# Sums with V in runs of four behind each key product, turned keys at the other end of memory, and seven banks for the mixer's output in one hybrid decoder step

## The chip, the cores and the metric

The kernel runs on one core of a Trainium2 chip. The metric is device time in microseconds (us), the median of several executions. Engines are named as in the profile: PE is TensorE, PEld its weight loads, DVE VectorE, ACT ScalarE, POOL GpSimd, SP SyncE, which here only issues DMAs. A page of the paged cache in this text means one gather of [128, 1024] floats (512 KB).

## The reference

One layer of a decoder for two request groups, 1024 prompt tokens and 8 samples of 8 new tokens each (64 more columns, 1088 together), all in float32. Cut to what matters for the change:

```python
h = x + 0.5 * rms_norm(swiglu(rms_norm(x)))                    # FFN1
q_sb, k_sb, v_sb, q_r, k_r, v_r, g_r, a_sb, a_r = split(rms_norm(h) @ w_in)
o_sb = stick_breaking(q_sb, k_sb, v_sb)                        # 8 heads x 64, strictly causal
o_r  = silu(g_r) * head_rms_norm(retention(rope(q_r), rope(k_r), v_r))
m = sigmoid(a_sb) * (o_sb @ w_sb_out) + sigmoid(a_r) * (o_r @ w_ret_out)
h = h + rms_norm(m @ w_o)
h = h + 0.5 * rms_norm(swiglu(rms_norm(h)))                    # FFN2

def sb_block(q, k, v, ...):        # a sample sees 2048 cached keys (16 pages of 128) and its new ones
    z = q k^T / 8 + bias
    log_stay = where(mask, log_sigmoid(-z), 0)
    a = where(mask, exp(log_sigmoid(z) + sum of log_stay of all later keys), 0)
    return a @ v
```

The samples' keys and values come through a page table from the pools `cache_k` and `cache_v`, 8 samples x 2048 keys x 512 floats each, 67 MB for both.

## The kernel before

Everything is kept with features on partitions and the 1088 tokens as columns. A dense product is done as three matmuls (`mm3`, L133, L137, L138), with each operand split into a high part (`hi`, L96, on ACT) and a low part (`lo`, L99, on DVE, for some weights on POOL). The program runs FFN1, the combined projection `w_in`, retention, the prompt's stick-breaking attention (`prompt_sb`), the samples' attention (`decode_sb`), the mixer's output (`mixer_out`) and FFN2.

**Samples' attention.** Four groups `g` of two samples (`b2`). For each group, blocks `j` of 512 cached keys are taken from last to first. `gather` (L1100, on POOL) brings two pages of keys per sample and block; they are turned on PE by 16 transposes (L1202, four per `m`) and copied by DVE or ACT (L1207, L1209) into `kt`, one of two tiles in pool `deck`. `product` (L1183, matmuls at L1115) multiplies them with the queries `qd`, which lie block by block in 32 columns with zeros between. `stick` (L1139 to L1158) makes the weights, `weights` (L1174) turns them on PE into `at`. `values` (L1226) then sums these with V: one call per 128 keys, two calls to a page of V. A call of `side_by_side` (L1111) is four matmuls on 32 columns each, which stand next to each other in the array, one per pair of heads; PE's instructions list a call as "32x128 x4", and the trace as one row of "128*32 ... x8" or more. Key products are such calls too, with 512 columns.

**What sets the order.** The code is written as generators, and each `yield` is a place where other work may be put. `both` takes a step of the keys of group g+1 and a step of the values of group g in turn, one V call to a step; `through` adds dense work at each step, `FILL_DEC` pieces of `fill` for each (`fill(1)` is one k of three matmuls). The dense work is what `a_r`'s gates and `o_r @ w_ret_out` need (L866, `ret_steps`, operands `uh`, `ul` and weights `wh`, `wl`). Its operands `ul` are loaded from `orT` in `ret_prep` (L843). A scheduler then places the instructions of each engine by their readiness and priority; three of a call's four matmuls have a high priority and follow the first. SP issues all plain DMAs in one order, and POOL all gathers, along with memsets and some low parts.

**Memory.** Pools are opened and closed like a stack. The pages lie in pool `decp`, the turned keys in `deck`, both opened after `prompt_sb` has closed all of its pools, the one of the prompt's keys and values (`pqk`) with them, and both closed before `mixer_out` opens its own.

**Mixer.** The outputs of both attentions lie in DRAM (`osT`, all 1088 columns, and `orT`). `mixer_out` (L1511) loads `osT` into `sq` (L1528) in chunks of 512, 288 and 288 columns, makes high and low parts, multiplies with `w_sb_out` into one of two banks "pa", and DVE multiplies by the gate `gaT` (L1542, L1545) and adds the retention's share `mrT` (L1544, L1546). The scheduler mixes these with the products by `w_o` (banks "pb"). The last lines of `decode_sb` store the samples' part into `osT` (L1275).

Of the kernel before, what the change touches and what calls it, by code (L numbers as in the profile page):

```python
# [43 lines left out]
FILL_DEC = (.6, .8, .8, .8, .6)  # L44
# [24 lines left out]
class Trunk:  # L69
# [99 lines left out]
    def setup(self):  # L169
# [17 lines left out]
        self.osT = self.t(self.dram, [512, T], "osT")  # L187
# [700 lines left out]
    def prompt_sb(self):  # L888
        nc, io = self.nc, self.io
        win = io["w_in"][0]  # L890
        with ExitStack() as ctx:
            qp = self.pool("pqk", ctx)
# [12 lines left out]
            def proj(p):  # L905

                qs = [self.t(qp, [P, TP], "qs", F32R, bufs=3) for e in range(2)]
                kh = [self.t(qp, [P, TP], "kh", F32R, bufs=3) for e in range(2)]
                kl = [self.t(qp, [P, TP], "kl", F32R, bufs=3) for e in range(2)]
                vs = [self.t(qp, [P, 8, P], "vs", F32R, bufs=3) for e in range(2)]  # L910
# [159 lines left out]
    def decode_sb(self):  # L1070
# [5 lines left out]
        with ExitStack() as ctx:  # L1076
            pp = self.pool("decp", ctx)
            kp_ = self.pool("deck", ctx)
            dp = self.pool("dec", ctx)
# [11 lines left out]
            kn = self.t(kp_, [P, 4, TD], "kn")  # L1091
# [13 lines left out]
            qd = self.t(kp_, [P, 288], "qd")  # L1105
            nc.gpsimd.memset(qd, 0.0)
            atns = [self.t(dp, [P, P], f"atn{x}") for x in range(2)]
            for x in range(2):
                nc.gpsimd.memset(atns[x][64:128], 0.0)

            def side_by_side(out, w, x, first, last):  # L1111
# [13 lines left out]
            def logits(g, ats):  # L1125


                qv = qd.rearrange("q (b x) -> q b x", x=144)[:, :, :P].rearrange("q b (m y) -> q b m y", y=32)
# [31 lines left out]
                def new_keys():  # L1160
# [4 lines left out]
                    bt = self.t(dp, [P, TD], "btn")  # L1165
# [5 lines left out]
                    nc.scalar.activation(atn[:TD], tp[:TD, :P], AF.Copy)  # L1171
# [11 lines left out]
                def product(ps, b2, j, kt):  # L1183
                    side_by_side(ps, partial(query, b2), lambda m: kt[:, m, :], b2 == 0, b2 == 1)
                    if b2:
                        bt = self.t(dp, [P, 512], "bt", bufs=2)
                        left[0] = stick(bt, ps.rearrange("q (h i x) -> q h x i", h=2, i=2), 512, left[0])
                        todo.append((j, bt))

                late, todo, left = [], [], [None]  # L1190
                nk = new_keys()
                step = 0
                for j in range(NG - 1, -1, -1):
                    ps = self.bank("pb")
                    for b2 in range(2):
                        kp = [gather(self.t(pp, [P, 1024], "page", bufs=6), ck, 2 * g + b2, 2 * j + x)
                              for x in range(2)]
                        kt = self.t(kp_, [P, 4, 512], "kt", bufs=2)
                        for m in range(4):
# [6 lines left out]
                            if m % 2:  # L1206
# [3 lines left out]
                            if late and m == 1:  # L1210
                                product(*late.pop(0))
                            if todo and b2 == 1:
                                weights(*todo.pop(0))
# [4 lines left out]
                        late.append((ps, b2, j, kt))  # L1218
                while late:
                    product(*late.pop(0))  # L1220
                yield
                while todo:
                    weights(*todo.pop(0))
                yield

            def values(g, ats):  # L1226
                po = self.bank("pm")
                for b2 in range(2):
                    out = po[:, b2 * P : (b2 + 1) * P]
                    for j in range(NG, -1, -1):  # L1230
                        for i in range(4 if j < NG else 1):
                            if j < NG and i % 2 == 0:
                                vp = gather(self.t(pp, [P, 1024], "vpage", bufs=5), cv, 2 * g + b2, 2 * j + i // 2)
# [3 lines left out]
                                               lambda m: src[:, m * P : (m + 1) * P], j == NG, j == 0 and i == 3)  # L1237
                            self.marks.append(ins.ins)
# [13 lines left out]
            def both(k, v):  # L1252
                for _ in range(2):
                    next(k)
                    yield
                done = False
                while not done:
                    done = True
                    for x in (k, v):
                        if next(x, x) is not x:  # L1260
# [573 lines left out]
```

## Time and profile before

| what | value |
|---|---|
| median of 3 runs | 2899.72 us (2897.93 to 2901.84) |
| profiled execution, its own time | 2891.72 us |
| its span | 2889.2 us |
| mean granted PE clock | 0.99 |
| PE busy | 2798.6 us, 97% |
| DVE, ACT, POOL busy | 70%, 43%, 26% |
| samples' attention | about 1641 to 1942 us |
| first mixer product | 1947.88 us |

The span is the time from the first to the last recorded instruction of the profiled execution; its own time is that of the same execution as the runs are timed, and differs from the median as executions differ. PE's matmuls are pipelined: one starts before the row of the one before it ends, so what a matmul costs is read from start to start, not from its length. PEclk is the share of PE's full clock that was granted in a stretch.

### The profile page before, as it was taken

What the parts mean: (1) busy time and instruction counts of PE and PEld (TensorE: products, weight loads), DVE (VectorE), ACT (ScalarE), POOL (GpSimd) and SP (SyncE); (2) the same over time, 40 slices, a digit from 0 to 9 for tenths busy, and PEclk for the clock granted to TensorE, in tenths of its full rate; (3) what the DMA queues carried; (4) which work ended last, traced back from release to release, by engine and by line L of the source; (5) the groups of instructions that cost most, each with busy time, mean ns of one, the idle gap of its engine ahead of it and who ended that gap; (6) DMA issues with size and microseconds to landing.
All of it is one profiled execution on the core that took longest, in us unless ns stands there. A gap on an engine that the chain in (4) does not pass through costs nothing.

```text
span 2889.2 us, 51617 instructions
## 1 busy us (share of the span) xinstructions
PE 2798.6 (97%) x20064; PEld 2633.3 (91%) x20064; DVE 2017.1 (70%) x3922; ACT 1245.3 (43%) x2546; POOL 738.5 (26%) x679
## 2 busy tenths in 40 slices
PE   7999999999999999999999889989999999999998
PEld 7898899999999999989999867768989988999997
DVE  7888878888753553546888744436578888688776
ACT  6444444444343333335666543213354444544443
POOL 0234513333150000000000245520013334233321
PEclk9999999999999999999999999999999999999999
DMA  6444444333252322333222389876333336333431
GB/s 177 145 127 144 140 155 123 110 112 108 80 162 83 99 84 86 94 113 80 76 74 76 123 294 332 297 244 198 105 96 121 119 110 189 122 103 107 130 89 42
DMA packets 420420, 380.63 MB, mean 132 GB/s; under 512 B 30352, under 2 KB 380944, under 8 KB 420176
## 3 DMA queue, kind: packets, MB, share of 16 engines
q1 hardware_dynamic: 397904, 306.03, 34.6%
q0 software_dynamic: 22272, 71.31, 7.4%
q8 instruction: 157, 2.57, 0.4%
q14 instruction: 87, 0.71, 0.1%
HBM read 310.03 MB, written 63.05 MB: 129 GB/s over the span
## 4 chain that ended last, share of the span: by engine, by line
PE 59%; DVE 5%; DMA 3%; issue 2%; POOL 1%; ACT 1%; SPq 0%; DVEq 0%; POOLq 0%; ACTq 0%
PE pa L133 10%; PE pa L138 10%; PE pa L137 10%; PE pb L133 3%; PE pb L138 3%; PE pb L137 3%; PE pc L137 3%; PE pc L138 3%; PE pc L133 3%; PE pc L1202 2%; PE pm L1011 1%; PE pm L1115 1%; PE pc L999 1%; DVE sl L99 1%; DMA ul<-orT 1%
## 5 line engine op out<-in xcount | busy, mean ns | idle before, releaser
L96 ACT ACTIVATE sh<-wr 128x512 fp32r<-128x512 f32 x592 | 340.0, 624 | 364.1 <-POOL wr L590 135.5
L133 PE MATMUL pa<-uh,wh 128*128 128x384 f32 (+1 forms) x1408 | 476.7, 339 | 4.2 <-ACT qdec L920 2.0
L138 PE MATMUL pa<-uh,wl 128*128 128x384 f32 (+1 forms) x1408 | 464.4, 330 | 0.0
L137 PE MATMUL pa<-ul,wh 128*128 128x384 f32 (+1 forms) x1408 | 463.5, 329 | 0.4 <-POOL ul L99 0.4
L99 DVE TENSOR_TENSOR sl<-wr,sh 128x512 fp32r<-128x512 f32 x592 | 398.8, 701 | 60.2 <-ACT sh L96 56.8
L133 PE MATMUL pa<-q,sh 128*128 128x256 f32 (+1 forms) x1408 | 410.4, 292 | 15.7 <-DVE p L648 7.8
L137 PE MATMUL pa<-q,sh 128*128 128x256 f32 (+1 forms) x1408 | 409.5, 291 | 2.2 <-DVE q L99 2.2
L138 PE MATMUL pa<-q,sl 128*128 128x256 f32 (+1 forms) x1408 | 408.5, 290 | 0.3 <-DVE sl L99 0.3
L137 PE MATMUL pc<-hl,whd 128*128 128x256 f32 (+2 forms) x1088 | 350.4, 324 | 2.6 <-DVE hl L99 2.6
L138 PE MATMUL pc<-hh,wld 128*128 128x256 f32 (+2 forms) x1088 | 350.0, 323 | 0.0
L133 PE MATMUL pc<-hh,whd 128*128 128x256 f32 (+2 forms) x1088 | 343.6, 324 | 4.5 <-DVE y L718 2.5
L718 DVE TENSOR_TENSOR y<-y,pc 128x256 f32<-128x256 f32 (+2 forms) x496 | 250.1, 516 | 135.8 <-PE pc L138 133.9
L133 PE MATMUL pb<-q,sh 128*128 128x288 f32 (+1 forms) x1088 | 314.8, 290 | 6.5 <-ACT sh L96 4.9
L138 PE MATMUL pb<-q,sl 128*128 128x288 f32 (+1 forms) x1088 | 314.6, 289 | 0.5 <-DVE sl L99 0.4
L137 PE MATMUL pb<-q,sh 128*128 128x288 f32 (+1 forms) x1088 | 314.9, 290 | 0.0
L133 PEld LDWEIGHTS pa<-q,sh 128*128 128x128 f32 x1408 | 268.2, 191 | 20.8 <-DVE p L648 8.8
L133 PEld LDWEIGHTS pa<-uh,wh 128*128 128x128 f32 x1408 | 265.7, 189 | 20.1 <-issue 10.0
L137 PEld LDWEIGHTS pa<-q,sh 128*128 128x128 f32 x1408 | 268.0, 190 | 4.7 <-DVE q L99 2.7
L137 PEld LDWEIGHTS pa<-ul,wh 128*128 128x128 f32 x1408 | 265.7, 189 | 3.3 <-issue 1.4
L138 PEld LDWEIGHTS pa<-q,sl 128*128 128x128 f32 x1408 | 267.2, 190 | 1.5 <-DVE sl L99 0.5
L138 PEld LDWEIGHTS pa<-uh,wl 128*128 128x128 f32 x1408 | 265.2, 188 | 2.7 <-issue 1.7
L588 POOL TENSOR_TENSOR wr<-wr 128x512 f32<-128x512 f32 x76 | 108.2, 1424 | 495.5 <-DVE sl L99 495.4
(340 smaller groups left out, 5958.3 us busy)
## 6 DMA issues: line engine op xcount, KB each, us to landing
wr<-in_w_ffn_gu_dram SPq DMA_DIRECT2D x176, 512.0 KB
wrd<-in_w_ffn_down_dram SPq DMA_DIRECT2D x88, 512.0 KB
wr<-in_w_in_dram SPq DMA_DIRECT2D x56, 512.0 KB
q<-cB SPq DMA_DIRECT2D x16, 576.0 KB
wr<-in_w_o_dram SPq DMA_DIRECT2D x10, 512.0 KB
cB<-y SPq DMA_DIRECT2D x32, 144.0 KB
cB<-xr SPq DMA_DIRECT2D x32, 144.0 KB
s<-in_state_ret_dram SPq DMA_DIRECT2D x16, 256.0 KB
```

What stands on the lines that cost most here:

```text
L96: return self.nc.scalar.activation(dst, src, AF.Copy)
L99: (eng or self.nc.vector).tensor_tensor(dst, src, hi.bitcast(F32), op=ALU.subtract)
L133: ins = mm(ps, wh, xh, start=first, stop=False)
L137: mm(ps, wh, xl, start=False, stop=False)
L138: mm(ps, wl, xh, start=False, stop=last)
L588: tt(v1, v0, v1, op=ALU.add)
L718: nc.vector.tensor_tensor(y[p][:, d, c], y[p][:, d, c], ps[:, :n], op=ALU.add)
L999: nc.tensor.transpose(tp[:, j * P : (j + 1) * P], bt[:, j * P : (j + 1) * P], self.ident)
L1011: ins = nc.tensor.matmul(po[:, lo:256], vs[:, j, :], ats[j // 4][x][:, j % 4, lo:256], start=(j == 0 and x == 0), stop=(j == last and x == 1))
L1115: return nc.tensor.matmul(out[32 * m : 32 * m + 32], w(m), x(m), start=first, stop=last, skip_group_check=True)
L1202: ins = nc.tensor.transpose(tp[:, i * P : (i + 1) * P], kp[i // 2][:, (i % 2) * 512 + m * P : (i % 2) * 512 + (m + 1) * P], self.ident)
```

## The change

The order of the work in the samples' attention is written anew. `values` yields once per four calls with V (two pages of V), and such a run is emitted by `logits` of the next group, straight behind the key product at `m == 1` (`next(others, None)`). `side_by_side` now chains all calls of a run (`run`), so that each packed matmul follows the one before. `FILL_DEC` is given anew, since steps are fewer. The last block of keys of the last group is finished in `last_block`, beside the last group's values.

The pages lie in pools `dec0` to `dec2`, which take the places of `pqk0` to `pqk2`, three pools for the prompt's heads in turn, so that each page waits for its own place only. `qd` is doubled, `atn` has 64 rows and `vnew` too, without memsets of the rest. The turned keys (`deck`) are opened at the other end of memory and stay open: their two tiles serve as the high and low parts of the mixer's first 512 columns, which `attn_parts` loads at the end of `last_block`. The samples' part of the output has a tensor of its own (`osD`). `mixer_out` makes the parts of chunk c+1 in the middle of chunk c, and its products go through seven banks in turn.

Of the diff, the pieces that move instructions:

```diff
-FILL_DEC = (.6, .8, .8, .8, .6)
+FILL_DEC = (1.6, 1.75, 2)
...
-        self.osT = self.t(self.dram, [512, T], "osT")
+        self.osT = self.t(self.dram, [512, TP], "osT")
+        self.osD = self.t(self.dram, [512, TD], "osD")
...
-            pp = self.pool("decp", ctx)
-            kp_ = self.pool("deck", ctx)
-            dp = self.pool("dec", ctx)
+            p0, p1, p2, dp = (self.pool(x, ctx) for x in ("dec0", "dec1", "dec2", "dec"))
+            key_pages = [(p2, f"kp{i}") for i in range(4)] + [(p0, f"kp{i}") for i in range(4, 6)]
+            value_pages = [(p1, f"vp{i}") for i in range(4)] + [(p0, "vp4")]
+            with self.tc.using_default_side("right"):
+                self.kpc = ExitStack()
+                kp_ = self.pool("deck", self.kpc)
+            key_parts = [(kp_, f"kt{i}") for i in range(2)]
...
-                ins = one(3)
-                with self.tc.high_priority():
-                    for m in (2, 1, 0):
-                        before, ins = ins, one(m)
-                        self.behind(ins, before.ins)
+                for m in (3, 2, 1, 0):
+                    if run:
+                        with self.tc.high_priority():
+                            ins = one(m)
+                        self.behind(ins, run[-1])
+                    else:
+                        ins = one(m)
+                    run.append(ins.ins)
...
-                            if m % 2:
+                            if m % 2 and (g or j < NG - 1):
...
-                            if late and m == 1:
-                                product(*late.pop(0))
+                            if m == 1:
+                                run.clear()
+                                if late:
+                                    late.pop(0)()
+                                next(others, None)
+                                run.clear()
...
+            def last_block():
+                late.pop(0)()
+                run.clear()
+                for _ in range(2):
+                    yield
+                todo.pop(0)()
                 yield
+                sh, sl = (in_turn(key_parts, [P, 4, 512], F32R) for _ in range(2))
+                self.first = sh, sl
+                self.attn_parts(sh, sl, 0, 512)
+                yield
...
+                        if j < NG:
                             self.marks.append(ins.ins)
                             yield
...
+            ats, others = {}, iter(())
             for g in range(4):
+                self.through(logits(g, ats, others), FILL_DEC[min(g, 1)])
+                ats, others = {}, values(g, ats)
+            self.through(both(last_block(), others), FILL_DEC[2])
             while self.tiles or self.live:
                 self.fill(1)
-            nc.sync.dma_start(self.osT.rearrange("(m q) t -> q m t", q=P)[:, :, TP:T], ost)
+            nc.sync.dma_start(self.osD.rearrange("(m q) t -> q m t", q=P), ost)
...
+                banks = ("pa", "pb", "pc", "pa", "pb", "pc", "pc")
...
-                        ps = self.bank("pa")
+                        if d == 4 and c < 2:
+                            on = mch[c + 1]
+                            sh[c + 1], sl[c + 1] = (self.t(op, [P, 4, on[1]], f"s{x}{c + 1}", F32R) for x in "hl")
+                            self.attn_parts(sh[c + 1], sl[c + 1], *on)
+                        ps = self.bank(banks[(8 * c + d) % 7])
```

PE, second group of samples, before: key product (`pb<-kt`, 512 columns) and calls with V (`pm<-vpage`) among the dense fill (`pa<-uh` and `pa<-ul`, 384 columns).

```order
L1115 MATMUL pm_20481<-vpage_20498,at_19922 32x128 x4
L133 MATMUL pa_20477<-uh_3629_19784,wh_20019 128x384
L137 MATMUL pa_20477<-ul_3630_19785,wh_20019 128x384
L138 MATMUL pa_20477<-uh_3629_19784,wl_20020 128x384
L133 MATMUL pa_20477<-uh_3629_19784,wh_20019 128x384
L1115 MATMUL pb_20184<-kt_20275,qd_19203 32x512 x4
L137 MATMUL pa_20477<-ul_3630_19785,wh_20019 128x384
L138 MATMUL pa_20477<-uh_3629_19784,wl_20020 128x384
L1115 MATMUL pm_20481<-vpage_20541,at_19922 32x128 x4
```

The same place after (`L1224` turns a page of keys `kp`, `L1129` is the packed matmul).

```order
L137 MATMUL pa_20267<-ul_3610_19731,wh_19738 128x320
L1201 MATMUL pc_20109<-ident_66,bt_20029 128x128 x4
L1224 MATMUL pc_20118<-ident_66,kp_3667_20097 128x128 x2
L1224 MATMUL pc_20118<-ident_66,kp_3668_20099 128x128 x2
L1129 MATMUL pb_20004<-kt_3653_20009,qd_3518_19218 32x512 x4
L1129 MATMUL pm_19834<-vp_3674_20128,at_19924 32x128 x8
L1129 MATMUL pm_19834<-vp_3675_20138,at_19924 32x128 x8
L1224 MATMUL pc_20154<-ident_66,kp_3667_20097 128x128 x2
L1224 MATMUL pc_20154<-ident_66,kp_3668_20099 128x128 x2
```

Three packed stretches between dense matmuls have become one, with a key product and four calls with V behind it; over the whole attention there are 105 such stretches in PE's order before and 47 after.

POOL, at the start of the samples' attention, before: `kl` are the last copies of the prompt's attention, `wl` low parts of weights, `page` and `vpage` the gathers.

```order
L950 DMA kl_17656<-kl_17656 64x256
L99 TENSOR_TENSOR wl_19147<-wr_19144,wh_19146 128x1024
...
L1100 DMA page_19314<-in_cache_k_dram,rowix_75 128x1024
L1100 DMA vpage_19719<-in_cache_v_dram,rowix_75 128x1024
...
L1100 DMA vpage_19901<-in_cache_v_dram,rowix_75 128x1024
L99 TENSOR_TENSOR wl_20020<-wr_20017,wh_20019 128x1024
L1106 MEMSET qd_19203 128x288
L1100 DMA page_19362<-in_cache_k_dram,rowix_75 128x1024
```

POOL at the same place after.

```order
L952 DMA kl_17661<-kl_17661 64x256
L1113 DMA kp_3522_19228<-in_cache_k_dram,rowix_75 128x1024
L1113 DMA kp_3523_19230<-in_cache_k_dram,rowix_75 128x1024
L1113 DMA kp_3534_19296<-in_cache_k_dram,rowix_75 128x1024
L1113 DMA kp_3535_19298<-in_cache_k_dram,rowix_75 128x1024
L99 TENSOR_TENSOR wl_19155<-wr_19152,wh_19154 128x1024
L1120 MEMSET qd_3517_19217 128x288
L1120 MEMSET qd_3518_19218 128x288
L1113 DMA kp_3544_19354<-in_cache_k_dram,rowix_75 128x1024
```

The first gathers now stand ahead of a low part, and the memsets of `qd` behind four gathers where before eleven stood ahead (six of K, five of V) with two low parts.

SP, from the attention to the mixer, before: `osT` is stored (L1275) and loaded again (L1528).

```order
L146 DMA wr_22958<-in_w_o_dram 128x8x128
L1275 DMA osT_79<-odec_19195 128x4x64
L1528 DMA sq_22306<-osT_79 128x512
L874 DMA mrT_84<-gs_22268 128x320
L1528 DMA sq_22310<-osT_79 128x512
L1528 DMA sq_22314<-osT_79 128x512
L1528 DMA sq_22318<-osT_79 128x512
L1542 DMA xr_22391<-gaT_81 128x512
```

SP at the same place after.

```order
L875 DMA mrT_85<-gs_22064 128x384
L1543 DMA kt_3991_22155<-osT_79 128x2x512 x2
L875 DMA mrT_85<-gs_22140 128x384
L875 DMA mrT_85<-gs_22225 128x320
L146 DMA wr_22927<-in_w_o_dram 128x8x128
L1581 DMA xr_22365<-gaT_82 128x512
...
L146 DMA wr_22991<-in_w_o_dram 128x8x128
L1581 DMA xr_22461<-gaT_82 128x512
L1303 DMA osD_80<-odec_19209 128x4x64
```

The prompt's 512 columns are loaded in two DMAs of 512 KB ahead of the last stores of the fill, and the samples' store stands behind five chunks' gate loads.

## Rows read from the trace of the kernel before

**Rows 1.** The page's first part: busy us, share of the span, instructions.
```profile
PE 2798.6 (97%) x20064; PEld 2633.3 (91%) x20064; DVE 2017.1 (70%) x3922; ACT 1245.3 (43%) x2546; POOL 738.5 (26%) x679
```

**Rows 2.** Stretches: length, busy PE PEld DVE ACT POOL, PEclk, DMA, GB/s.
```profile
1653.70:1668.00 14.30, 10.68 (x85) 8.04 (x83) 3.64 (x10) 3.72 (x11) 6.40 (x6) 0.88 0.85 312
1655.00:1660.00 5.00, 1.95 (x16) 1.56 (x15) 0.45 (x1) 1.01 (x6) 2.58 (x2) 0.79 1.03 415
1668.00:1700.00 32.00, 29.84 (x258) 20.97 (x253) 17.30 (x31) 14.87 (x29) 15.55 (x15) 0.95 0.88 289
1700.00:1760.00 60.00, 54.33 (x545) 42.95 (x543) 31.11 (x54) 25.64 (x50) 33.02 (x29) 1.00 0.94 330
1760.00:1820.00 60.00, 60.00 (x586) 44.14 (x585) 23.61 (x45) 16.38 (x30) 31.03 (x31) 1.00 0.88 298
1820.00:1880.00 60.00, 60.00 (x588) 44.03 (x590) 28.88 (x44) 16.11 (x31) 33.35 (x32) 1.00 0.89 310
1942.00:1948.00 6.00, 0.12 (x1) 0.12 (x1) 1.71 (x3) 0.63 (x1) 0.00 (x0) 0.72 0.90 292
1948.00:1990.00 42.00, 41.68 (x193) 34.52 (x194) 25.70 (x46) 11.96 (x23) 0.00 (x0) 0.96 0.60 190
```

**Rows 3.** PE's timeline, one call with V: start us, us, operation.
```profile
1891.85 0.34 PE L137 MATMUL pa<-ul,wh 128*128 128x384 f32 x1
1892.02 0.33 PE L138 MATMUL pa<-uh,wl 128*128 128x384 f32 x1
1892.29 0.42 PE L1115 MATMUL pm<-vpage,at 128*32 128x128 f32 x8
1892.64 0.44 PE L133 MATMUL pa<-uh,wh 128*128 128x384 f32 x1
1892.92 0.34 PE L137 MATMUL pa<-ul,wh 128*128 128x384 f32 x1
```

**Rows 4.** PE's timeline, two calls with V in a row.
```profile
1928.34 0.34 PE L138 MATMUL pa<-uh,wl 128*128 128x384 f32 x1
1928.61 0.65 PE L1115 MATMUL pm<-vpage,at 128*32 128x128 f32 x16
1929.19 0.44 PE L133 MATMUL pa<-uh,wh 128*128 128x384 f32 x1
```

**Rows 5.** PE's timeline, a V call and a key product.
```profile
1889.09 0.42 PE L1115 MATMUL pm<-vpage,at 128*32 128x128 f32 x8
1889.33 1.04 PE L1115 MATMUL pb<-kt,qd 128*32 128x512 f32 x8
```

**Rows 6.** PE's waits, 1640 to 2020 us: us in total, times, longest.
```profile
PE pa L133 <- ACT sh L96: 7.6, 1, 7.6
PE pc L1115 <- POOL qd L1106: 3.1, 1, 3.1
PE pc L1179 <- DVE bt L1157: 3.0, 1, 3.0
PE pc L1202 <- DVE at L1180: 2.0, 1, 2.0
...
PE pc L1202 <- ACT btn L1152: 1.4, 1, 1.4
PE pc L1115 <- ACT kt L1209: 1.1, 1, 1.1
PE pm L1115 <- DMA vpage<-in_cache_v_dram,rowix: 0.8, 1, 0.8
```

**Rows 7.** Tile `ul`, 1640 to 1760 us: ScalarE's idle time until it landed (us, times).
```profile
  DMA ul<-orT: 18.5, 9
```

**Rows 8.** VectorE by shape, 1942 to 2024 us: busy, mean ns; idle before, releaser.
```profile
L1545 DVE TENSOR_TENSOR xr<-xr,pa 128x288 f32<-128x288 f32 x16 | 7.3, 454 | 9.3 <-PE pa L138 9.1
```

**Rows 9.** Gathers of key pages (tile `page`): issue to landing.
```profile
DMA to landing us min/median/max: 4.3/6.1/9.6
```

More of the change, by code (lines that the diff above doesn't have):

```diff
@@ L891, in prompt_sb @@
         with ExitStack() as ctx:
-            qp = self.pool("pqk", ctx)
+            places = [self.pool(f"pqk{i}", ctx) for i in range(3)]
             sp = self.pool("pst", ctx)
@@ L905, in proj @@
             def proj(p):
[L907 to L910, printed above, removed]
+                at = [places[(2 * p + e) % 3] for e in range(2)]
+                qs = [self.t(x, [P, TP], "qs", F32R) for x in at]
+                kh = [self.t(x, [P, TP], "kh", F32R) for x in at]
+                kl = [self.t(x, [P, TP], "kl", F32R) for x in at]
+                vs = [self.t(x, [P, 8, P], "vs", F32R) for x in at]
                 for e in range(2):
@@ L1102, in gather @@
                 return t
-            qd = self.t(kp_, [P, 288], "qd")
-            nc.gpsimd.memset(qd, 0.0)
-            atns = [self.t(dp, [P, P], f"atn{x}") for x in range(2)]
+            qds = [self.t(p0, [P, 288], f"qd{x}") for x in range(2)]
             for x in range(2):
-                nc.gpsimd.memset(atns[x][64:128], 0.0)
+                nc.gpsimd.memset(qds[x], 0.0)
+            atns = [self.t((p0, dp)[x], [TD, P], f"atn{x}") for x in range(2)]
+            run = []
             def side_by_side(out, w, x, first, last):
@@ L1187, in product @@
                         left[0] = stick(bt, ps.rearrange("q (h i x) -> q h x i", h=2, i=2), 512, left[0])
[L1188 to L1190 removed]
+                        todo.append(partial(weights, j, bt))
+                left = [None]
                 nk = new_keys()
@@ L1217, in logits @@
                             yield
-                        late.append((ps, b2, j, kt))
-                while late:
-                    product(*late.pop(0))
+                        late.append(partial(product, ps, b2, j, kt))
+                next(others, None)
+            def last_block():
+                late.pop(0)()
+                run.clear()
+                for _ in range(2):
+                    yield
+                todo.pop(0)()
                 yield
-                while todo:
-                    weights(*todo.pop(0))
+                sh, sl = (in_turn(key_parts, [P, 4, 512], F32R) for _ in range(2))
+                self.first = sh, sl
+                self.attn_parts(sh, sl, 0, 512)
                 yield
@@ L1252, in both @@
             def both(k, v):
-                for _ in range(2):
-                    next(k)
+                for x in chain.from_iterable(zip(k, v)):
+                    run.clear()
                     yield
[L1256 to L1260, printed above, removed]
-                            done = False
-                            yield
-            ats = {}
-            self.through(logits(0, ats), FILL_DEC[0])
-            for g in range(4):
-                if g < 3:
-                    new = {}
-                    self.through(both(logits(g + 1, new), values(g, ats)), FILL_DEC[1 + g])
-                    ats = new
-                else:
-                    self.through(values(g, ats), FILL_DEC[4])
+                for x in v:
+                    run.clear()
+                    yield
+            ats, others = {}, iter(())
+            for g in range(4):
+                self.through(logits(g, ats, others), FILL_DEC[min(g, 1)])
+                ats, others = {}, values(g, ats)
+            self.through(both(last_block(), others), FILL_DEC[2])
             while self.tiles or self.live:
                 self.fill(1)
-            nc.sync.dma_start(self.osT.rearrange("(m q) t -> q m t", q=P)[:, :, TP:T], ost)
+            nc.sync.dma_start(self.osD.rearrange("(m q) t -> q m t", q=P), ost)
     def retention(self):
@@ L1508, in mixer_in, with attn_parts @@
                 self.decode_sb()
+    def attn_parts(self, sh, sl, o, n):
+        lf = sl.bitcast(F32)
+        m = min(n, TP - o)
+        for q in range(0, 4, 2):
+            qq = slice(q * P, (q + 2) * P)
+            self.nc.sync.dma_start(lf[:, q : q + 2, :m], self.osT[qq, o : o + m].rearrange("(k p) t -> p k t", p=P))
+            if m < n:
+                self.nc.sync.dma_start(lf[:, q : q + 2, m:], self.osD[qq, :].rearrange("(k p) t -> p k t", p=P))
+        for q in range(4):
+            self.hi(sh[:, q, :], lf[:, q, :])
+            self.lo(sl[:, q, :], lf[:, q, :], sh[:, q, :])
     def mixer_out(self):
```

36 lines of the change are left out of this document (17 added, 19 removed).

## The prediction

> **What bounds the kernel now.** The totals say TensorE: PE is busy for 97% of the span [rows 1]. That share is an average, so the stretch that the change touches comes next, by the table of stretches [rows 2]. All instructions before the samples' attention and all behind the mixer's output product stand in the same order before and after; only what runs from about 1641 us to some 2020 us moves. There PE has whole stretches without a gap (60.00 of 60 us twice) and three that are not full: 10.68 of 14.30 us at the start, 54.33 of 60 in 1700 to 1760, and 0.12 of 6 us at 1942, between the attention and the mixer. DMA stands at 298 to 330 GB/s all along, a share of 0.88 to 0.94. So the time is PE's time plus PE's pauses, and the question is what the change does to each, and whether DMA then has room.
>
> Third, the timeline of PE, since "busy" hides one cost. A dense matmul comes every 0.17 us (1891.85 to 1892.02) [rows 3]. One call with V, which is four packed matmuls on 32 columns each (eight records), stands between two dense ones: from 1892.02 to the next dense one but one at 1892.92 are 0.90 us, and without the call it would be two times 0.17. The call costs 0.55 us. With two calls in a row the first dense start behind them is 0.85 us off (1928.34 to 1929.19) [rows 4], with one 0.62 (1892.02 to 1892.64): a further call costs 0.23. So each stretch of packed work has a fixed price of 0.55 - 0.23 = 0.32 us for going over to 32 columns and back. Where a V call is followed at once by a key product, the product starts 0.24 us behind it [rows 5], which is the price of a call alone: between two packed calls nothing is switched.
>
> Fourth, PE's list of waits over 1640 to 2020 us [rows 6]: 7.6 us before the mixer's first product, on the high parts of the attention's output, and 3.1, 3.0, 2.0, 1.4 and 1.1 us inside the attention; one wait of 0.8 us for a page of V. The middle three and the 1.1 lie where the retention's `ul` loads land: ScalarE sat idle for 18.5 us in 9 waits for them [rows 7], with the copies of turned keys, weights and `btn` queued behind.
>
> **The change part by part.**
>
> *Runs of four.* PE's order holds the same work in both kernels (512 turns, 744 dense fill matmuls, 32 key products, 128 calls with V), but its packed calls stand in 105 stretches before and in 47 after: most of after's are one key product and four V calls. 58 fewer stretches by 0.32 us: **-18.6 us**. This is bounded below by nothing saved, if what a stretch pays were paid by each call (rows 4 and 5 speak against), and above by 58 x 0.55 = 32 us, which would need that further calls cost nothing; I take the timeline's split.
>
> *Pauses inside the attention.* The 3.1 us are the first query product waiting for the `qd` memset, which stands on POOL behind a weight unit's low part (L99) and eleven gathers. After, four gathers stand ahead of that low part and both `qd` memsets right behind it; the early gathers are possible since the pages lie on memory that head 5 leaves, not on that which the whole of the prompt's attention leaves. The 3.0, 2.0, 1.4 and 1.1 us come from the `ul` loads. They stay in the program, but after holds 201 dense fill matmuls per 128 turns in the first group where before had 69, so PE has some 22 us (132 x 0.17) more of its own work to run beside them. Of the sum of 10.6 I take 8.1 as gone and 2.5 as staying: **-8.1**.
>
> *The seam.* Before, the samples' part of `osT` is stored behind the last sum, and the mixer's loads of `osT` stand behind that store on SP; hence the 7.6 us. After, the prompt's 512 columns are loaded into the key tiles that the last key product has freed, and their store and load are no longer one tensor with the samples' (`osD`). Behind that product PE still has 35 dense matmuls (6.0 us) and eight V calls in three stretches (2.8 us), 8.8 us in all. A page, which is of the same 512 KB as one such load, lands in 4.3 us at best and 6.1 in the median [rows 9]; two loads and the first high part (some 0.7 us) come to 5 to 8. So the wait goes, just: **-7.6**. Its bounds are 0 gained (loads land as late as 9.6 and the parts queue behind other work) and 7.6.
>
> *The clock.* Where PE paused, the granted clock was 0.88 over 10.68 us of work, 0.95 over 29.84, and 0.96 over 41.68 at the mixer's start [rows 2]; at 1.00 that work takes 1.3, 1.5 and 1.7 us less. With the pauses go **-4.0** of these 4.5.
>
> *What it costs.* First, DMA. The pages (128 of 512 KB, 67 MB) and the rest have to come in less time. In 1700 to 1880 us DMA moved 330, 298 and 310 GB/s [rows 2], 56.3 MB in 180 us; if those groups shrink to some 167 us, they want 337. Between 1655 and 1660, when gathers were queued with nothing ahead of them, 415 GB/s went through. I put 2 us on it. Second, a run of four takes two whole pages of V at once, and the second of them must have been issued two runs earlier to be there: the places (five for V, six for keys) allow that, and each is freed by the run as a whole. I take nothing here, and price it below. Third, the mixer. With three more banks in turn, VectorE can trail PE by seven products instead of two, but it starts late, since its `xr` loads now lie on memory of the V pages. Before, VectorE waited for PE there (9.1 us before the narrow evacuations alone [rows 8]), so it has slack; a narrow product is 12 matmuls of an estimated 0.13 us (0.17 x 288/384) or some 1.6 us, and its four VectorE operations of 0.45 us come to 1.8 where before the output products stood between. Over 16 narrow products that is 3 us more than PE's time, of which the seven banks swallow most; 0 to 5, taken as 1. DMA and this are **+3**.
>
> *No longer needed:* the memset of `vnew`'s lower half and of `atn` on POOL, which ran beside PE. Nothing. The first eight copies of turned keys all go to ScalarE where VectorE took half, while PE has dense fill to run; nothing.
>
> **Sum.** -18.6 - 8.1 - 7.6 - 4.0 + 3 = -35.3 us. The profiled execution took 2891.7 us (span 2889.2), so 2856; the median of the runs shown is 2899.7, 8 us above it. Against that median, as the time will be given, it is 2864 us. The terms' own bounds (switches 15 to 20, pauses 5 to 10.6, seam 3 to 7.6, clock 2 to 4.5, costs 0 to 9) make 2851 to 2874.
>
> **Rivals.**
>
> *Transfers become the bound.* Then 1700 to 1880 can't shrink as forecast. At 330 GB/s, the best of the three stretches, 56.3 MB take 171 us against the 167 that I need, and 4 us of the sum are lost; at their mean of 313 nothing of those 180 us is saved, and 13 are lost. For it: a DMA share of 0.94 where 330 GB/s were reached. Against it: the 415 GB/s, and that PE waited for a page once, for 0.8 us, so the rates of before are what was asked for rather than what could be had. Time 2868 to 2877, and as the key and value pages of the first group press too, say 2874. Chance 0.14.
>
> *The pauses come back elsewhere.* The `ul` loads still come between, and ScalarE now has all of the first eight copies of turned keys and `btn`. If all 10.6 us and the clock's 4 stay, 2864 + 8.1 + 4.0 = 2876. Chance 0.13.
>
> *Only one edge of a stretch has a price.* The row mechanism: of the 0.32 us some lie in going to 32 columns and some in the first dense weight load behind; were only the first saved when calls are joined, at 0.18 us a stretch, 58 stretches give 10.4 and the time is 2872. Against it: in rows 5 no edge of either sort is seen between joined calls. The Trainium skill, "TensorEngine Tiling (Array Packing)", section Key Properties, says that a change of the tiling mode drains TensorE, and "TensorE: Matmul & The Clock Gate", section Single matmul latency, puts the drain at about 175 ns; by that figure a stretch would cost an estimated 0.18 us if one drain is meant and 0.35 if both edges drain, and the trace's 0.32 agrees with the second. Chance 0.05.
>
> *Pages of V come late, and it is slower.* One mechanism: POOL issues a run's second page only when a place is freed, and a place is freed only by a whole run. If the second page is asked for one run ahead instead of two, it stands on POOL behind two key gathers (2 us, at 1.0 us each by 31.03 us in 31 [rows 2]) and lands 6.1 us later [rows 9]: 8.1 us, where from the end of one run to the start of the next some 6 us of PE work stand (18 dense matmuls and 12 turns by 0.17 are 5.1, weights the rest). About 24 runs would then each be late, and PE stops with them, since the next turns and dense products stand behind the run in PE's queue: at 2 us each, 48 us, less the 35 gained, or 2912 us. It decides from 1.5 us per run up. Against it: the places in the order given make it two runs, some 14 us, well over the 9.6 us of the slowest landing. Chance 0.04.
>
> That the change doesn't do what it says is settled by the order of PE: the runs, the early gathers and the preloaded tiles are there.
>
> **How the numbers follow.** The forecast has 0.64, the rivals 0.14, 0.13, 0.05 and 0.04. The measurement can tell about 0.2%, 5.8 us: faster means under 2893.9. All but the last end there with a margin of 14 us and more, and of it I leave 0.02 to a mix of half-late pages and lost clock that ends within 0.2%: faster 0.94, same 0.02, slower 0.04. The range that holds the time 8 times in 10 takes the forecast's lower end less 2 us, since the switch might be worth up to 0.36, and reaches to the upper ends of the first two rivals with 5 us for both at once: 2849 to 2885.
>
> **What would show it.** Right: V stands in runs of eight packed matmuls and more on PE, one dense start to the next over a run of K and four V calls being the sum of the calls plus 0.32; no wait over 1 us before the first mixer product; the granted clock at 0.99 or 1.00 from 1660 on; 335 GB/s and more in the middle of the attention. Wrong: a row of waits of PE for pages of V or of keys (the first or the last rival, by their number); ScalarE's waits for `ul` passed on to PE as before; VectorE ahead of PE's waits in the mixer, with the banks full; or a stretch's price of about 0.5 us that shows up behind each run.

## The result, and the profile after

The changed kernel took 2867.4 us in the median (2862.5 to 2873.8, 4 runs) where the one before took 2900.1 us (2897.9 to 2901.8, 4 runs): ratio 0.989, 95% interval 0.987 to 0.991. The forecast was 2864 us. Measured again beside the later experiments the ratio was 0.990 (0.988 to 0.992). The kernel before itself stood at 2892 to 2894 us in the three later comparisons, so each experiment is read as a ratio to the runs of before beside it.

The profiled execution of after took 2862.5 us (span 2860.0), 29.2 us less than that of before. PE's busy time, by the page's first part:

```profile
PE 2779.8 (97%) x20064; PEld 2638.2 (92%) x20064; DVE 2012.3 (70%) x3918; ACT 1244.4 (44%) x2550; POOL 737.5 (26%) x677
```

PE has the same 20064 records and is busy for 18.8 us less [rows 1]. The stretches, which answer to [rows 2] (same columns: length, busy time and count of PE, PEld, DVE, ACT, POOL, granted clock, DMA share, GB/s):

```profile
1650.00:1690.00 40.00, 40.00 (x288) 35.30 (x287) 18.42 (x35) 21.98 (x45) 16.72 (x13) 1.00 0.80 263
1690.00:1700.00 10.00, 7.11 (x50) 5.72 (x49) 6.83 (x15) 4.47 (x11) 3.08 (x4) 1.00 1.02 341
1700.00:1760.00 60.00, 60.00 (x638) 49.91 (x637) 28.88 (x48) 19.89 (x37) 35.77 (x33) 1.00 0.88 308
1760.00:1820.00 60.00, 59.46 (x651) 50.36 (x650) 26.67 (x47) 16.97 (x32) 34.27 (x32) 1.00 0.92 331
1820.00:1880.00 60.00, 59.62 (x629) 50.82 (x633) 28.13 (x50) 17.84 (x29) 30.06 (x30) 1.00 0.94 336
1930.00:1950.00 20.00, 14.51 (x79) 13.14 (x78) 18.21 (x35) 8.09 (x17) 0.00 (x0) 0.83 0.80 253
1950.00:1990.00 40.00, 40.00 (x234) 35.97 (x234) 21.92 (x47) 13.30 (x23) 0.00 (x0) 1.00 0.66 203
```

In 1700 to 1880 PE gets 1918 records through where before had 1719. From 1650 to 1690 us PE has no gap and the full clock. One stretch is new: 1930 to 1950 us, 14.51 of 20 us at a mean clock of 0.83, inside the mixer. PE's waits from 1640 to 2020 us say what it is (us in total, times, longest), beside [rows 6]:

```profile
PE pb L133 <- ACT sh L96: 5.5, 1, 5.5
PE pc L1224 <- DVE at L1202: 2.9, 1, 2.9
PE pc L1001 <- DVE bt L1052: 1.4, 1, 1.4
PE pm L1129 <- issue: 0.9, 2, 0.5
PE pc L1280 <- ACT od L1277: 0.6, 1, 0.6
PE pm L1129 <- DMA vp<-in_cache_v_dram,rowix: 0.2, 1, 0.2
```

The waits for `qd`, `btn`, `kt`, for the samples' `bt` and before the first mixer product are gone (L1001 is the prompt's attention). One behind the `ul` loads stays (2.9, at 1697), and 5.5 us before the mixer's second chunk (`pb`, 1940.8 us) are new. The chain of waits leads there (start us, us, what):

```profile
1922.55 0.62 PE pm L1129 x16
...
1923.25 0.04 ACT od L1277
...
1923.57 1.07 ACT who L96
...
1925.91 0.69 DVE xr L1584
...
1933.12 4.50 DMA xr<-gaT
...
1939.79 0.63 ACT mh L96
1940.42 0.34 ACT sh L96
...
1940.81 0.61 PE pb L133
```

Read from the top: the last sum with V ends, is copied (`od`), then ScalarE and VectorE split a weight of w_o, and only then VectorE gates the first mixer product (1925.91), 22 us after PE began it (1903.8). Before that VectorE was idle for 16.8 us, until the copies of the last sums (`odec`), which stand first in its queue, could run:

```profile
1924.05 0.39 DVE L1285 COPY odec<-pc 64x32 f32<-64x32 f32 x2 [16.80 <-PE pc L1280]
```

The gate loads of later products wait for places that it frees, and the second chunk's high part `sh` stands on ScalarE behind the first chunk's `mh`.

For all kernels the same piece can be cut out: from the end of the last sum of the prompt's attention on PE to the end of the last w_o product. "Waits" are PE's gaps over 0.1 us in it, "rest" what is left. Behind its waits PE ran at a granted clock of 0.5, the lower of its two levels (1.2 GHz); half of its busy time there is what the lower level cost, the column "clock", and is part of the rest. All of it comes from the traces. The stretches at the lower level in before, and the one in after (columns as above):

```profile
1657.90:1661.30 3.40, 3.00 (x19) 2.65 (x19) 0.00 (x0) 1.00 (x4) 0.81 (x1) 0.50 0.71 278
1678.40:1681.80 3.40, 3.40 (x33) 2.51 (x32) 2.31 (x6) 0.94 (x3) 2.44 (x3) 0.50 0.89 325
1944.60:1951.40 6.80, 3.52 (x8) 2.77 (x9) 2.72 (x4) 2.53 (x4) 0.00 (x0) 0.50 1.05 376
```

```profile
1937.90:1944.80 6.90, 3.99 (x17) 3.99 (x18) 6.84 (x14) 4.03 (x10) 0.00 (x0) 0.51 1.02 327
```

| kernel | packed stretches | piece, us | waits | rest | clock |
|---|---|---|---|---|---|
| before | 105 | 448.7 | 20.1 | 428.6 | 5.0 |
| bv4_before_runs_of_four | 62 | 449.6 | 31.4 | 418.2 | 9.2 |
| bv4_carried | 67 | 433.9 | 16.7 | 417.2 | 5.5 |
| after | 47 | 417.5 | 10.1 | 407.4 | 2.0 |
| after_again | 47 | 417.7 | 9.7 | 408.0 | 3.8 |
| v1_single_calls | 106 | 431.4 | 6.3 | 425.2 | 2.0 |
| runs_apart | 60 | 427.9 | 15.0 | 412.9 | 4.1 |
| seam_undone | 39 | 429.1 | 18.9 | 410.2 | 7.5 |
| parts_early | 47 | 416.3 | 8.3 | 407.9 | 1.7 |
| evac_first | 47 | 417.9 | 11.5 | 406.4 | 2.0 |
| two_banks | 42 | 419.8 | 10.4 | 409.4 | 6.1 |
| late_pages | 47 | 414.2 | 6.6 | 407.6 | 2.7 |
| late_pages_parts_early | 47 | 415.6 | 8.2 | 407.5 | 0.0 |

From before to after: 31.2 us, 10.0 of them waits and 21.2 rest; of the rest 3.0 are clock (5.0 less 2.0), which leaves 18.2 for 58 stretches.

### The profile page after: what moved, and what is told of

Its sections match the earlier page's. It is cut to its first block, busy times and chain, and to the rows that moved or that the text cites. A ratio compares the mean times of both kernels' runs of the same rounds, so it can differ in the third digit from the quotient of the medians.

```text
span 2860.0 us, 51596 instructions
## 1 busy us (share of the span) xinstructions
PE 2779.8 (97%) x20064; PEld 2638.2 (92%) x20064; DVE 2012.3 (70%) x3918; ACT 1244.4 (44%) x2550; POOL 737.5 (26%) x677
## 4 chain that ended last, share of the span: by engine, by line
PE 61%; DVE 4%; DMA 2%; issue 1%; POOL 1%; ACT 0%; SPq 0%; DVEq 0%; ACTq 0%; POOLq 0%
PE pa L133 10%; PE pa L138 10%; PE pa L137 10%; PE pb L133 4%; PE pb L138 4%; PE pb L137 4%; PE pc L137 3%; PE pc L138 3%; PE pc L133 3%; PE pc L1224 2%; PE pm L1013 1%; PE pm L1129 1%; PE pb L1129 1%; PE pc L1001 1%; DVE sl L99 1%
```

## The experiments

**after_again.** No edit. 

> The changed kernel unchanged, beside the next three and the kernel before on one chip, as their measure: 0.987 to 0.991 of before.

2862.5 us, 0.990 (0.988 to 0.992). The expected ratio; the experiments are compared with it.

**v1_single_calls: is it the stretches?**

```diff
+                            if j < NG and g < 3 and i < 3:
+                                yield
                         if j < NG:
...
-                            if m == 1:
-                                run.clear()
-                                if late:
-                                    late.pop(0)()
-                                next(others, None)
-                                run.clear()
+                            run.clear()
+                            if late and m == 1:
+                                late.pop(0)()
+                            next(others, None)
+                            run.clear()
```

> The changed kernel with V's calls of groups 0 to 2 given one per step instead of four behind a key product; pages, banks, seam and fill stay. PE's order has 106 packed stretches instead of 47. Theory (each stretch has a price of 0.32 us): 59 x 0.32 = +19 us against the changed kernel, so some 2886 us and 0.995 of the kernel before; start to start over a single V call 0.55 us more than the dense matmuls alone. Rival (the gain came from pauses and early loads, a stretch's price is hidden): within 5 us of the changed kernel. Rival (only one edge has a price, 0.18): +11 us.

2880.4 us, 0.996 (0.995 to 0.998). Two thirds of the gain are gone. The waits are fewer than after's, so none of it is a wait: rest is 425.2 against 407.4, 17.8 us for 59 stretches, 0.30 us each, at the same loss of clock. The theory holds; 0.18 would have given 11.

**bv4_before_runs_of_four: runs alone, on the kernel before.**

```diff
-FILL_DEC = (.6, .8, .8, .8, .6)
+FILL_DEC = (.6, 1.25, 1.25, 1.25, 2.2)
...
+                        if j < NG:
                             self.marks.append(ins.ins)
                             yield
...
-                done = False
-                while not done:
-                    done = True
-                    for x in (k, v):
-                        if next(x, x) is not x:
-                            done = False
-                            yield
+                for i, _ in enumerate(k):
+                    yield
+                    if i % 4 == 0 and next(v, v) is not v:
+                        yield
+                for _ in v:
+                    yield
```

> The kernel before with one part of the change alone: four calls with V to a step, every fourth step of the keys, and all four chained; nothing else. 62 packed stretches instead of 105. Theory: 43 x 0.32 = -14 us, so 2886 us, 0.995, with the waits for qd (3.1), at the ul loads and before the mixer (7.6) still there. Rival (pages of V come late when two are taken at once, with the old places): PE waits for vpage, slower than before by up to 20 us. Rival (no price of a stretch): unchanged.

2894.7 us, 1.000 (0.999 to 1.002): a miss, nothing was gained. PE's waits and one place of its timeline (start us, us, operation, idle before it):

```profile
PE pc L1186 <- DVE bt L1162: 11.3, 3, 5.4
PE pa L137 <- DVE sl L99: 6.2, 1, 6.2
PE pc L1115 <- POOL qd L1106: 3.1, 1, 3.1
...
PE pm L1115 <- DMA vpage<-in_cache_v_dram,rowix: 0.9, 1, 0.9
```

```profile
1781.02 0.71 PE L1186 MATMUL pc<-ident,bt 128*128 128x128 f32 x4 [2.96 <-DVE bt L1162]
```

Rest fell by 10.4 us, 0.24 a stretch; without the 4.2 us more that the lower clock behind the new waits took it would be 14.6, 0.34 a stretch. But waits rose by 11.3, of which 8.3 are for `bt`: at the ends of the first three groups the weights' transposes stand right behind the key product whose weights they turn, and the V calls that had lain about there were already done. Pages were not late. The kernel before has one such place, at the end of its first group, with the same wait:

```profile
1707.13 0.71 PE L1179 MATMUL pc<-ident,bt 128*128 128x128 f32 x4 [2.96 <-DVE bt L1157]
```

**bv4_carried: the same, with the last block carried into the next group.** `late` and `todo` live across groups as in the changed kernel, and `qd` is doubled.

```diff
-                while late:
-                    product(*late.pop(0))
-                yield
-                while todo:
-                    weights(*todo.pop(0))
-                yield
+                if g == 3:
+                    while late:
+                        late.pop(0)()
+                    yield
+                    while todo:
+                        todo.pop(0)()
+                    yield
```

> The kernel before with runs of four V calls as in bv4_before_runs_of_four, and one thing more: the last key product of a group and its weights are carried into the next group's first steps (two qd in turn), so that the weights don't stand right behind the product they wait for at the end of groups 1 and 2. 67 packed stretches instead of 105. Theory (bv4's gain of about 14 us was eaten by 11.3 us of waits for bt at group ends and their clock): those waits are gone or under 3 us, and the time is 38 x 0.32 = 12 us under before, 0.995 to 0.997. Rival (runs without a key product ahead bring no gain, the price of a stretch is not 0.32 here): within 4 us of before again, with the waits gone.

2881.5 us, 0.996 (0.995 to 0.998). Its waits begin with

```profile
PE pc L1214 <- DVE kt L1219: 3.8, 2, 2.9
PE pa L133 <- ACT sh L96: 3.2, 1, 3.2
PE pa L137 <- DVE sl L99: 2.8, 1, 2.8
```

and none is for `bt` in the samples' attention. Rest is 11.4 us under before for 38 stretches, 0.30 each. So the runs gain here once something stands between a product and its weights at the ends of the groups.

**runs_apart: the run two steps behind the product.**

```diff
                                 if late:
                                     late.pop(0)()
+                                run.clear()
+                            if m == 3:
+                                run.clear()
                                 next(others, None)
                                 run.clear()
```

> The changed kernel with the runs of four given two steps behind the key product instead of right behind it; all else stays. 60 packed stretches instead of 47, and the weights' transposes lose the run as cover behind their product. Theory: 13 x 0.32 = +4 us, and waits of PE for bt (weights behind the product) if the run was the cover: up to 2 us in each of 14 blocks; +4 to +15 us in all. Rival (fill covers the weights anyway): +4 us and no new waits.

2874.5 us, 0.994 (0.993 to 0.995), 0.004 over after_again, some 12 us. Rest is up 4.9 us on after_again for 13 stretches (0.37 each, but the kernels with 47 stretches differ among themselves by 1.6 us) and waits by 5.3:

```profile
PE pb L133 <- ACT sh L96: 5.5, 1, 5.5
PE pa L133 <- ACT kt L96: 3.5, 1, 3.5
PE pc L1201 <- DVE bt L1178: 2.6, 1, 2.6
PE pb L1129 <- DVE kt L1229: 2.1, 1, 2.1
```

The half on stretches holds. Of the other half little does: there is one wait for `bt` in 14 blocks, in the last one, so in the others the fill covers the weights, as the rival said. The order also moves the last products and so the mixer's first high parts (3.5).

**seam_undone: the mixer's first loads behind the samples' store.**

```diff
-                self.attn_parts(sh, sl, 0, 512)
...
                 sh[0], sl[0] = self.first
+                self.attn_parts(*self.first, 0, 512, self.stored.ins)
...
+            if stored is not None:
+                self.behind(ld, stored)
```

> The changed kernel with the loads of the mixer's first 512 columns held behind the samples' store on SP, as before the change; tiles, banks and runs stay. Theory (the early loads hide 7.6 us and more): PE has no work left while the sums end, are stored (2 us), loaded (5 us) and split (0.7 us), a wait of 8 to 11 us, less 8 stretches that are joined in the last group (2.6 us) and less some of the 5.5 us wait in the mixer, as VectorE is then no longer late: net +1 to +6 us. Rival (the seam is worth its whole 7.6 us and clock): +8 to +12 us. Rival (loads are hidden anyway): no wait over 2 us before the first mixer product.

2878.0 us, 0.994 (0.993 to 0.996), some 13 us over after_again (the piece is 11.5 us longer): more than expected, the rival's size, by another way. Waits, and two stretches:

```profile
PE pm L1129 <- DMA vp<-in_cache_v_dram,rowix: 7.6, 7, 2.5
PE pa L133 <- ACT kt L96: 6.9, 1, 6.9
```

```profile
1910.00:1930.00 20.00, 7.75 (x122) 4.03 (x114) 3.72 (x7) 2.32 (x3) 3.83 (x5) 0.62 0.80 281
1930.00:1950.00 20.00, 16.70 (x61) 13.35 (x62) 12.40 (x23) 7.27 (x15) 0.00 (x0) 0.78 0.75 218
```

With nothing else to do PE reaches the last V pages before they land (7.6 us), then waits for the loads (6.9), and works on at a mean clock of 0.62 and 0.78. The early loads thus hide two things: their own landing, and the last pages', since the mixer's products fill the time between the last sums. The wait in the mixer (5.7 in after_again) is absent here, so the 11.5 us are what is left of these 14.5 and of the lost clock.

**parts_early, evac_first: what is the 5.5 us wait?** Two edits from two sides. parts_early:

```diff
-                        if d == 4 and c < 2:
+                        if d == 0 and c < 2:
...
+                        if c == 0 and d == 2:
+                            self.behind(ld, self.part.ins)
```

> The changed kernel with the loads and high and low parts of the mixer's columns 512 to 799 asked for at the start of the first chunk instead of its middle, and kept ahead of the gate loads of the third product on SP. Theory (the 5.5 us wait in the mixer is the high part of the second chunk standing on ACT behind seven high parts of gated products, which wait for VectorE): that wait goes, and with it some 2 us of lowered clock: -5 to -8 us against the changed kernel, 2860 us, 0.986. Rival (VectorE's late start is the bound, and the seven banks are full at that point): the wait moves to a bank (PE waiting for DVE's xr), gain 0 to 2 us.

2863.0 us, 0.991 (0.989 to 0.992), within the interval of after. The wait for `sh` is gone and others stand in its place:

```profile
PE pa L133 <- DVE xr L1586: 1.7, 1, 1.7
PE pb L133 <- DVE xr L1586: 1.5, 1, 1.5
...
PE pb L133 <- ACT y L1603: 0.7, 1, 0.7
...
PE pc L133 <- DVE xr L1586: 0.5, 1, 0.5
```

The rival holds: PE now waits for banks that VectorE has not emptied. evac_first puts VectorE's first gatings ahead in its queue (`self.copies` holds the copies of the last group's sums):

```diff
+                        if c == 0 and d == 2:
+                            for x in self.copies:
+                                self.behind(x, ins.ins)
+                            gate = {mybir.EngineType.DVE: ins.ins, mybir.EngineType.Activation: hi.ins}
...
-                ws[d] = unit(d)
+                self.beside(lambda: ws.__setitem__(d, unit(d)), tuple(gate), gate)
```

> The changed kernel with VectorE's gating of the mixer's first three products put ahead of the copies of the last samples' sums and of the first low parts of w_o, and the fifth V page laid under the third product's loads. Theory (VectorE starts 18 us late, since copies that wait for the last sums stand first in its queue, and everything late in the mixer follows from it): VectorE starts at 1912 to 1920 instead of 1925 us, the waits of the mixer and the low clock behind them go: -5 to -8 us against the changed kernel. Rival (the loads of gates, not VectorE's queue, come late): VectorE starts within 2 us of where it did, gain 0 to 2.

2863.1 us, 0.989 (0.987 to 0.991), no gain. The first gate load on SP, and VectorE's first gating:

```profile
1905.93 0.32 SPq L1586 DMA_DIRECT2D xr<-gaT  x1
```

```profile
1916.51 0.69 DVE L1589 TENSOR_TENSOR xr<-xr,pa 128x512 f32<-128x512 f32 x1 [11.33 <-DMA xr<-gaT]
1922.60 0.69 DVE L99 TENSOR_TENSOR ml<-xr,mh 128x512 fp32r<-128x512 f32 x1 [4.06 <-ACT mh L96]
```

VectorE does start 9 us earlier, as the theory had it, but only after 11.3 idle us that end with a load that took 10.6 us from issue to use. Then it is idle for 4.1 us more for the high part `mh`, since on ScalarE `od`, which waits for the last sum, still stands ahead (1921.66). PE's wait for `sh` is 8.7 us instead of 5.5, since the second chunk's loads come still later on SP (from 1938.3 us, in after from 1934.7). So one queue was opened, and the transfers and ScalarE's queue were next. Where the mixer's floor lies was not found.

**two_banks: what the seven banks are worth.**

```diff
-                banks = ("pa", "pb", "pc", "pa", "pb", "pc", "pc")
+                banks = ("pa",) * 7
```

> The changed kernel with the mixer's products in the two banks pa alone instead of seven in turn. Theory (seven banks let TensorE run ahead of a VectorE that starts late): TensorE stops after two products and ends its products with VectorE instead of some 5 us ahead of it, +4 to +8 us, in waits for xr. Rival (VectorE's total work bounds anyway, banks only move the wait): within 2 us.

2867.5 us, 0.991 (0.989 to 0.993); the piece is 2.1 us longer. That is between the two expectations and not told from nothing. The program's order answers the lack of banks: products by w_o move in between (first one at 1936.6 us, in after_again at 1966.8), and the waits are now for V pages (4.0 us), for `xr` (2.0) and at the copies of the sums.

**late_pages: do the first pages of keys have to come early?**

```diff
-            key_pages = [(p2, f"kp{i}") for i in range(4)] + [(p0, f"kp{i}") for i in range(4, 6)]
-            value_pages = [(p1, f"vp{i}") for i in range(4)] + [(p0, "vp4")]
+            key_pages = [(p1, f"kp{i}") for i in range(4)] + [(p0, f"kp{i}") for i in range(4, 6)]
+            value_pages = [(p2, f"vp{i}") for i in range(4)] + [(p0, "vp4")]
```

> The changed kernel with the first key pages laid under the place of the prompt's last heads (the V pages' place) and V's under that of head 5, so that the first gathers can't start before the prompt's attention ends. Theory: first turned page some 10 us later, dense fill is used up there and missing later, DMA has 10 us less: +2 to +6 us, in new waits at the ul loads. Rival (fill hides it): within 2 us, as after has 201 fill products in the first group.

2860.8 us, 0.988 (0.986 to 0.990). The edit does less than its expectation says. Keys and V change places, but gathers go out as early as in after: ten stand ahead of the prompt's last sum (1653.4 us), the first four for V and not for keys.

```profile
1570.39 1.78 POOL L1113 DMA_INDIRECT vp<-in_cache_v_dram,rowix  x1 [0.53 <-PE pb L1034]
1653.91 0.93 POOL L1113 DMA_INDIRECT kp<-in_cache_k_dram,rowix  x1 [13.31 <-PE pm L1013]
```

The first page is turned 7.0 us behind that sum (1660.4), where after turns it 6.4 us ahead of it, and nothing is lost: no wait for `qd`, none at the `ul` loads (waits 6.6 against 9.7), and a piece 3.4 us shorter than after_again's. The rival holds; the expected +2 to +6 is not seen. What the early gathers as a whole are worth no run shows.

**late_pages_parts_early: the two together.** 

> The two edits late_pages and parts_early together on the changed kernel, as a candidate. Theory: each took one wait away in its profile (3 us at the ul loads, 5.5 us before the second chunk, of which 3 to 4 came back as waits for banks): -3 to -6 us against the changed kernel, 0.986 to 0.989 of before, which the interval can't tell from it surely. Rival: the waits only move, within 2 us.

2860.0 us, 0.988 (0.987 to 0.990): faster than before, not told from after.

## Why the prediction was right or wrong

**Runs of four, -18.6: right.** From before to after it is 18.2 us for 58 stretches, 0.31 each. With the clock taken out in the same way v1_single_calls gives 0.30, bv4_carried 0.31 and bv4_before_runs_of_four 0.34; runs_apart, with only 13 stretches, gives 0.25 beside after and 0.35 beside after_again. The forecast's 0.32 came from two places of the timeline. By the Trainium skill's drain of about 175 ns ("TensorE: Matmul & The Clock Gate", Single matmul latency), which that section gives for a single matmul, an estimate was 0.18 for one drain and 0.35 for two; the sums measured lie nearer two. Both edges of a stretch do have a price, but not the same one: by [rows 3] the lone call starts 0.27 us behind the dense matmul ahead of it, 0.10 over the usual 0.17, and the other 0.22 lie behind it. What the forecast didn't name is the condition: bv4_before_runs_of_four has the runs without cover at the ends of the groups and gains nothing.

**Waits inside the attention, -8.1: right in size, wrong in one reason.** `qd`, `btn`, `kt` and the one on `bt` went, the one behind the `ul` loads stayed at 2.9, where 2.5 was taken. But the 3.0 us on `bt`, which I put down to the `ul` loads, were the weights right behind their own key product (1707.13 us, above): ScalarE and VectorE had no `ul` work between the two. They went since the last block is now carried into the next group, as bv4_carried shows. The early gathers, which I gave as one reason why the `qd` wait goes, were taken away by no run: late_pages only changes what the first four of them fetch. ScalarE's idle time for `ul` fell from 18.5 [rows 7] to 9.0 us.

**The seam, -7.6: right, and more hangs on it.** The wait is gone. In the changed kernel taking the early loads away costs 13 us, with the mixer's wait that goes along with them already taken off, since the mixer's products also cover the last pages.

**The mixer's cost, taken as 1 of the +3: mis-sized.** This is the term that failed: of 3 us that VectorE needs more than PE "the seven banks swallow most". PE's wait of 5.5 us came instead, just over the 0 to 5 that the text allowed for, and two_banks can't tell the seven banks' worth from nothing. I had priced VectorE's work for each product, and named the `xr` loads as what makes it start late, but not the copies that stand first in its queue and ScalarE's and wait for the last sum: it began 22 us late. What bounds the mixer stays open: parts_early took the wait for `sh` away and evac_first opened VectorE's queue, and neither gained time that the runs can tell.

**The clock, -4.0: three quarters.** Before lost 5.0 us (4.5 by the means of [rows 2]); after loses 2.0, behind the new wait. So -3.0. The sign "0.99 or 1.00 from 1660 on" failed there, at 0.51.

**DMA, taken as 2 of the +3: nothing.** 331 and 336 GB/s were moved, above the best of before over such a length, at a share of 0.92 to 0.94, and PE waited 0.2 us for pages. The first rival fell with that, and the last too: no page came late in runs of four. Only at the end are pages near to setting the pace, as the 7.6 us of seam_undone show.

Together: -18.2 for switches and -3.0 for the clock; -7.7 (10.6 less 2.9) and -7.6 for waits, +5.5 for the mixer and -0.2 for small waits. That is -31.2 in the piece, against the 29.2 by which the profiled executions differ and 32.7 between the medians. The forecast's -35.3 had 4.5 us too little on the mixer, 1 too much on the clock, and 2 for DMA that were not needed. That two of these errors cancel in part is luck, and the time came nearer to 2864 us than its terms deserve.

One sum of the prediction is wrong: the bounds of its terms add up to gains of 16.0 to 42.7 us, or 2857 to 2884 us from the median of before, and not to the 2851 to 2874 from which its range was drawn. The measured time lies in both.

## What to carry to other kernels

When a small operation in another shape is strewn among dense matmuls, read the price of a single one and of two in a row from start to start: the price of a single one, less what a second one adds, is what a stretch costs before any work, and joining calls saves just that. Where that takes away what stood between a product and the step that waits for its result, put something else there, or the gain comes back as a wait. And where work is brought forward across a seam, look at the first instructions in the queues of the engines behind it: once a wait is removed on one engine, what stands late on the next can become the new wait.

## What the runs showed that was not expected

Nothing is lost when the first page is turned 13 us later (late_pages). A gate load of 256 KB took some 10 us from issue to use while pages were in flight (evac_first, at a DMA share of 1.02), where a page of 512 KB landed in 6.1 in the median before [rows 9].
